# A first mixture of experts whose narrow experts use column halves of the array for the two halves of the weights' columns, with a new class of 32 slots on column quarters

## The chip, the core and the metric

The program runs on one core of one Trainium2 chip. The metric is the device time of one execution in microseconds (us). The times shown are a median of several executions; one more execution was taken with the hardware profiler, and all rows below come from it. TensorE (PE) multiplies, VectorE (DVE), ScalarE (ACT) and GpSimd (POOL) work on elements, SyncE (SP) issues the weight transfers.

## The reference, cut to the first mixture

Three transformer blocks follow each other on 256 tokens of width 1024. The change concerns the mixture of experts of the first: 32 experts, each token goes to its 4 best.

```python
def moe_ffn(h, w_router, b_router, w_mlp1, b_mlp1, w_mlp2, b_mlp2):
    logits = (h @ w_router).astype(jnp.float32) + b_router.astype(jnp.float32)
    top_v, top_i = lax.top_k(logits, TOP_K)                 # 4 of 32 experts
    gates = jax.nn.softmax(top_v, axis=-1)
    ...
    def expert_block(args):
        xb, e = args
        u = xb @ w_mlp1[e] + b_mlp1[e]                      # 1024 -> 2048
        x_glu = jnp.minimum(u[..., ::2], SWIGLU_LIMIT)
        x_lin = jnp.clip(u[..., 1::2], -SWIGLU_LIMIT, SWIGLU_LIMIT)
        a = x_glu * jax.nn.sigmoid(SWIGLU_ALPHA * x_glu) * (x_lin + 1)
        return a @ w_mlp2[e] + b_mlp2[e]                    # 1024 -> 1024
    ...
    out = jnp.zeros((T + 1, D), jnp.float32).at[slot_tok].add(ys.astype(jnp.float32) * slot_gate[:, None])
```

## The kernel before

`moe1` sorts the experts by their number of tokens on the chip (`Order.make`): place 0 is always expert 0, so that its weights can be fetched before routing is known; places 1 to 31 hold the others by falling count. A place has a fixed number of slots: 128 for the first 5 places (wide), 64 for the others (narrow). Should a count exceed its slots, `overflow1` runs a loop over all experts behind a branch.

Each expert has 12 weight tiles of 1 MB (128 x 2048 in fp32): 8 for the up product (two halves of 4) and 4 for the down product. A tile holds two k chunks j of 128 rows with 1024 columns each, and is used as the streamed operand in two column halves n of 512. The gathered tokens x (and later the activations a) are the loaded operand, so an expert with 64 slots fills 64 of the array's 128 columns. In `products` a narrow expert puts the even k chunk on columns 0 to 63 and the odd one on 64 to 127; the two partial sums land on the two halves of the partitions of one PSUM bank, one bank for each n. In `Expert1.act` the result is copied to SBUF (L1562, L1563) and multiplied by `K.fold`, two stacked identities, which transposes it and adds the two partial sums (L1571); a wide expert is transposed plainly (L548). Then comes `swiglu`. `rows` scales the down product by the gate and splits it into yh (L1600) and yl (L1601), and `scatter` multiplies them by the one-hot matrix st (L1330, L1331) and adds the product to the tokens' rows (L1333, L1336), one column half and one half of the tokens at a time.

The experts run in groups: (0), then four groups of one wide and two narrow places, then the rest by fours. For each group `gather` collects the tokens of all its experts by one-hot products (L1292, L1293), during the last expert of the group before. The order on PE, DVE and ACT is written out by hand in `moe1` (a manual schedule): up half 0 of expert e, the last two down tiles of e-1, up half 1, the first two down tiles; `step()` puts one piece of a gather or scatter between two weight tiles, `advance()` puts the next piece of an activation chain between tiles and into the middle of a tile; `weave_all()` finishes what is left at the end of a group. In this stage PSUM has two banks each for u, y, t and the general x.

Weights come through a ring of 12 slots (4 + 4 + 4). SP issues them in program order; each waits until TensorE has used what its slot held. For experts after 0, SP needs the expert's number, which `Order.make` gives at about 228 us. After the last expert the ring shrinks to 4, tiles of the next stage are prefetched, and two of them are split by ACT and DVE (L166, L167) ahead of the last yh.

The order of the groups and the product of a tile stand so before:

```python
WIDE, NARROW, WIDES = 128, 64, 5
CAPS = [WIDE] * WIDES + [NARROW] * (E1 - WIDES)
GROUPS = ([(0,)] + [(n, WIDES + 2 * n - 2, WIDES + 2 * n - 1) for n in range(1, WIDES)]
          + [tuple(range(n, min(n + 4, E1))) for n in range(3 * WIDES - 2, E1, 4)])
```

Of the kernel before, what the change touches and what calls it, by code (L numbers as in the profile page):

```python
# [9 lines left out]
F32 = mybir.dt.float32  # L10
F32R = mybir.dt.float32r
# [3 lines left out]
ALU = mybir.AluOpType  # L15
# [7 lines left out]
P = 128  # L23
# [852 lines left out]
class Residual:  # L876
# [46 lines left out]
    def add(self, x, k):  # L923

        for j in range(2):
# [9 lines left out]
GATHER = 2 * WIDE  # L935
EXTRA = 4


def host2(i):
# [7 lines left out]
    p[:, 34:98] = np.tile(np.eye(64, dtype=np.float32), (2, 1))  # L947
# [193 lines left out]
class Order:  # L1141
# [20 lines left out]
    def make(self, K, tmp, R, b1):  # L1162
# [35 lines left out]
        nc.vector.tensor_scalar(cap, pos, float(CAPS.count(WIDE)), float(WIDE - NARROW), op0=ALU.is_lt, op1=ALU.mult)  # L1198
        nc.vector.tensor_scalar_add(cap, cap, float(NARROW))
# [72 lines left out]
def gather(K, pool, pk, tok, caps, out):  # L1272
# [34 lines left out]
    for e0 in range(0, len(caps), 2):  # L1307
# [5 lines left out]
        for e, cap in some:  # L1313
            slot = K.iota64 if cap == NARROW else K.iota_p
# [6 lines left out]
def scatter(K, out, st, yh, yl):  # L1321

    nc = K.nc
    was = None
    for t in range(2):
        for n in range(2):
            ps = K.bank()
            c = slice(512 * n, 512 * n + 512)
            s = st[:, 128 * t:128 * t + 128]
            nc.tensor.matmul(ps, s, yh[:, c], start=True, stop=False)  # L1330
            nc.tensor.matmul(ps, s, yl[:, c], start=False, stop=True)  # L1331
            if was:
                nc.vector.tensor_add(*was)  # L1333
            was = out[:, t, c], out[:, t, c], ps
            yield
    nc.vector.tensor_add(*was)  # L1336


def moe1(K, x, sums, wr, rp, b1, fill, A2, sh2, gt2, gpost, banks, man, then):
    nc, tc, a = K.nc, K.tc, K.a  # L1340
    with ExitStack() as cs:
        rt = cs.enter_context(tc.tile_pool(name="route", bufs=1))
        out = rt.tile([P, 2, D], F32, name="moe")
        K.fold, K.iota64 = rp[:, 34:98], rp[:, 98:99]
# [175 lines left out]
class Expert1:  # L1520
# [4 lines left out]

    def __init__(self, K, pool, x, gs, b1, cap, advance, w1, w2):
        self.K, self.pool, self.x, self.gs, self.b1, self.cap = K, pool, x, gs, b1, cap
        self.advance, self.w1, self.w2 = advance, w1, w2
        self.parts = P // cap
        self.a = pool.tile([P, KD * WIDE], F32, tag="a", name="a")[:, :KD * cap].rearrange("p (k s) -> p k s", k=KD)  # L1530
        self.acting, self.rowed = set(), False

    def products(self, out, x, q, w):

        m, cap = self.parts, self.cap
        w = w.rearrange("p (k n) -> p k n", k=2)
        for n in range(2):
            for j in range(2):
                k = 2 * q + j
                r = slice(cap * (k % m), cap * (k % m) + cap)  # L1540
                self.K.nc.tensor.matmul(out[n][r], x[:, k], w[:, j, 512 * n:512 * n + 512], start=k < m, stop=k >= KD - m)  # L1541
            if n == 0:
                self.advance()
# [1528 lines left out]
```

## Time and profile before

| what | value |
|---|---|
| median of 3 runs | 2399.83 us (2399.82 to 2401.52) |
| profiled execution | 2405.79 us, span 2403.9 us, mean granted clock 0.972 |
| PE busy | 2291.6 us (95%) |
| DVE busy | 1230.2 us (51%) |
| ACT busy | 814.1 us (34%) |
| read from HBM | 675.82 MB, of which 384 tiles of 1 MB are this mixture's weights |

The profile gives busy time per engine, but the end of a matmul is modelled, so a busy PE is not PE at its peak. The mixture's experts take from about 200 to 1290 us of the span. To see what sets its pace one asks the trace for stretches of it (busy times, granted clock, share and rate of the DMA engines), for who waited for whom, and for the starts of one instruction that each expert has once or twice.

### The profile page before, as it was taken

The numbers are of one execution on the slowest core, as the hardware profiler recorded it, in microseconds if no ns is written. First come the engines' busy times: TensorE is split into PE (matmuls) and PEld (weight loads), VectorE is DVE, ScalarE is ACT, GpSimd is POOL, SyncE is SP. The second block draws the span as 40 slices with busy tenths as digits, with TensorE's granted clock in tenths as the row PEclk, the third lists the DMA queues.
The fourth block names the chain that finished last, engine by engine and source line by source line (L and its number), as shares of the span: only waits on it lengthen the run. The fifth ranks groups of instructions, "written<-read, shape, count | busy, mean of one in ns | idle before, by whom it ended". The sixth has DMA issues, their size and how long they took to land. (4 is left out here: it accounts for less than half of the span.)

```text
span 2403.9 us, 32504 instructions
## 1 busy us (share of the span) xinstructions
PE 2291.6 (95%) x12558; PEld 1449.9 (60%) x12558; DVE 1230.2 (51%) x2303; ACT 814.1 (34%) x1389; POOL 152.9 (6%) x202
## 2 busy tenths in 40 slices
PE   8899999999999999999998888999999998999997
PEld 5775444444443434343435866997889996666664
DVE  5782222222233333323236987887648556566675
ACT  3642010101111111111114674444545435555662
POOL 4000100000000000000000001001000001000000
PEclk8999999999999999999998988999999998999998
DMA  7674898979899999999994523676424445867782
GB/s 273 231 279 190 313 384 302 390 295 360 327 369 423 412 423 405 423 402 423 414 419 168 184 94 144 245 272 257 145 104 177 173 148 215 326 246 278 291 304 90
DMA packets 97845, 680.17 MB, mean 283 GB/s; under 512 B 11776, under 2 KB 14080, under 8 KB 16144
## 3 DMA queue, kind: packets, MB, share of 16 engines
q1 hardware_dynamic: 94752, 671.00, 71.9%
q0 software_dynamic: 2352, 6.44, 0.9%
q8 instruction: 103, 1.69, 0.3%
q10 hardware_dynamic: 576, 0.53, 0.1%
q14 instruction: 62, 0.51, 0.1%
HBM read 675.82 MB, written 2.11 MB: 282 GB/s over the span
## 5 line engine op out<-in xcount | busy, mean ns | idle before, releaser
L1541 PE MATMUL bank<-w,xg 128*64 128x512 f32 (+1 forms) x2048 | 547.1, 601 | 0.0
L167 DVE TENSOR_TENSOR whl<-w,whl 128x1024 fp32r<-128x1024 f32 (+1 forms) x337 | 400.3, 1206 | 175.9 <-ACT whl L166 175.2
L166 ACT CAST whl<-w 128x1024 fp32r<-128x1024 f32 (+1 forms) x347 | 350.5, 1039 | 242.8 <-PE bank L417 100.6
L1541 PEld LDWEIGHTS bank<-w,xg 128*64 128x64 f32 (+1 forms) x2048 | 176.9, 146 | 294.2 <-issue 262.0
L1541 PE MATMUL bank<-w,a 128*64 128x512 f32 (+1 forms) x1024 | 287.4, 605 | 0.0
L1563 DVE COPY us<-bank 128x512 f32<-128x512 f32 x64 | 44.3, 692 | 334.1 <-PE bank L1541 334.1
L1562 ACT COPY us<-bank 128x512 f32<-128x512 f32 x64 | 37.5, 586 | 485.3 <-PE bank L1541 485.3
L1541 PEld LDWEIGHTS bank<-w,a 128*64 128x64 f32 (+1 forms) x1024 | 80.4, 144 | 110.2 <-issue 97.0
L2926 PE MATMUL bank<-whl,xg 128*128 128x512 f32 x512 | 140.8, 404 | 2.1 <-DVE whl L167 2.1
L415 PE MATMUL bank<-hh,whl 128*128 128x256 f32 x448 | 129.1, 288 | 0.0
L417 PE MATMUL bank<-hh,whl 128*128 128x256 f32 x448 | 126.9, 284 | 2.1 <-DVE whl L167 2.1
L416 PE MATMUL bank<-hl,whl 128*128 128x256 f32 x448 | 126.8, 283 | 0.0
L1571 PEld LDWEIGHTS bank<-route_p,us 128*128 128x128 f32 x864 | 100.8, 191 | 42.5 <-issue 36.0
L1620 POOL TENSOR_SCALAR ss<-ss 128x256 f32<-128x256 f32 (+1 forms) x64 | 60.5, 946 | 951.6 <-ACT ss L1617 951.5
L1333 DVE TENSOR_TENSOR moe<-moe,bank 128x512 f32<-128x512 f32 x96 | 65.7, 688 | 105.4 <-PE bank L1331 104.9
L306 DVE SCALAR_TENSOR_TENSOR acc<-w,siluc,acc 128x256 f32<-128x256 f32 x234 | 115.0, 499 | 4.5
L2950 PE MATMUL bank<-w,s 128*64 128x512 f32 x256 | 116.7, 598 | 0.4 <-DVE s L2943 0.4
L417 PE MATMUL bank<-xh,whl 128*128 128x256 f32 x400 | 112.0, 280 | 2.0 <-DVE whl L167 2.0
L415 PE MATMUL bank<-xh,whl 128*128 128x256 f32 x400 | 112.2, 281 | 0.8 <-ACT xh L1834 0.8
L2926 PEld LDWEIGHTS bank<-whl,xg 128*128 128x128 f32 x512 | 89.3, 188 | 38.2 <-DVE whl L167 9.4
L416 PE MATMUL bank<-xl,whl 128*128 128x256 f32 x400 | 112.1, 281 | 0.2 <-DVE xl L1835 0.2
L1571 PE MATMUL bank<-route_p,us 128*128 128x64 f32 x864 | 107.5, 278 | 0.0
(719 smaller groups left out, 3895.9 us busy)
## 6 DMA issues: line engine op xcount, KB each, us to landing
w<-w_mlp SPq DMA_DIRECT2D x384, 1024.0 KB, 9.5
w<-w SPq DMA_DIRECT2D x96, 1024.0 KB, 5.6
w<-w_ada SPq DMA_DIRECT2D x48, 1024.0 KB, 5.0
w<-w_in SPq DMA_DIRECT2D x48, 1024.0 KB, 4.8
w<-w_ff SPq DMA_DIRECT2D x32, 1024.0 KB, 4.8
w<-w_out SPq DMA_DIRECT2D x12, 1024.0 KB, 4.9
w<-cmp_w SPq DMA_DIRECT2D x4, 1024.0 KB, 4.8
w<-w_ret_o SPq DMA_DIRECT2D x4, 1024.0 KB, 4.8
```

Of the source, the lines that this page charges most:

```text
L166: nc.scalar.copy(h, src)
L167: (eng or nc.vector).tensor_tensor(l, src, h.bitcast(F32), op=ALU.subtract)
L306: nc.vector.scalar_tensor_tensor(acc, wv[:, k], self.c[:, k:k + 1], acc, op0=ALU.mult, op1=ALU.add)
L415: nc.tensor.matmul(out, w.h[k][:, c], x.h[:, k], start=first and k == 0, stop=False)
L416: nc.tensor.matmul(out, w.h[k][:, c], x.l[:, k], start=False, stop=False)
L417: nc.tensor.matmul(out, w.l[k][:, c], x.h[:, k], start=False, stop=last and k == nk - 1)
L1333: nc.vector.tensor_add(*was)
L1541: self.K.nc.tensor.matmul(out[n][r], x[:, k], w[:, j, 512 * n:512 * n + 512], start=k < m, stop=k >= KD - m)
L1571: nc.tensor.matmul(ps[:, c], part, K.fold, start=True, stop=True)
L1620: nc.gpsimd.tensor_scalar_min(s, s, 1.0 / (1.0 + math.exp(-1.702 * 7.0)))
L2926: nc.tensor.matmul(self.u, x, part[k], start=q == 0 and k == 0 and n == 0, stop=q == 1 and k == 3 and n == 1)
L2950: nc.tensor.matmul(self.y[n], self.s[:, k], w[:, k, 512 * n:512 * n + 512], start=k == 0, stop=k == 1)
```

## The change

It does four things. In `Expert1.product` a narrow expert puts the column half n = 0 of the weights on columns 0 to 63 of the array and n = 1 on 64 to 127, both with the same k chunk, so that one bank holds everything: partitions 0 to 63 the first 512 columns and 64 to 127 the second. No partial sums are left to add, and the fold becomes a plain transpose. Places 16 to 31 get 32 slots (slim): they use four column quarters, two column halves times two k parities, and a fold by `K.fold32`. `scatter` handles both column halves in a step, for narrow and slim experts with 64 rows each of the contraction. And the groups become (slim, narrow, wide, slim) and (slim, narrow, narrow, slim) in turn, with the last one (slim, narrow, slim).

```diff
-WIDE, NARROW, WIDES = 128, 64, 5
-CAPS = [WIDE] * WIDES + [NARROW] * (E1 - WIDES)
-GROUPS = ([(0,)] + [(n, WIDES + 2 * n - 2, WIDES + 2 * n - 1) for n in range(1, WIDES)]
-          + [tuple(range(n, min(n + 4, E1))) for n in range(3 * WIDES - 2, E1, 4)])
+WIDE, NARROW, SLIM = 128, 64, 32
+WIDES, NARROWS = 5, 11
+CAPS = [WIDE] * WIDES + [NARROW] * NARROWS + [SLIM] * (E1 - WIDES - NARROWS)
...
+    w, n, s = (iter([p for p in range(1, E1) if CAPS[p] == c]) for c in (WIDE, NARROW, SLIM))
+    out = [(0,)]
+    for kinds in [(s, n, w, s), (s, n, n, s)] * 4:
+        out.append(tuple(p for k in kinds for p in [next(k, None)] if p is not None))
...
-    p[:, 34:98] = np.tile(np.eye(64, dtype=np.float32), (2, 1))
+    p[:, 34:98] = np.kron(np.eye(2), np.tile(np.eye(32), (2, 1)))
...
 def scatter(K, out, st, yh, yl):
...
-    was = None
+    was = []
+    halves = yh.shape[-1] < D
     for t in range(2):
+        s = st[:, 128 * t:128 * t + 128]
+        ps = [K.bank() for _ in range(2)]
+        for i, y in enumerate((yh, yl)):
+            for n in range(2):
+                if halves:
+                    r = slice(64 * n, 64 * n + 64)
+                    nc.tensor.matmul(ps[n], s[r], y[r], start=i == 0, stop=i == 1)
+                else:
+                    nc.tensor.matmul(ps[n], s, y[:, 512 * n:512 * n + 512], start=i == 0, stop=i == 1)
         for n in range(2):
-            ps = K.bank()
             c = slice(512 * n, 512 * n + 512)
-            s = st[:, 128 * t:128 * t + 128]
-            nc.tensor.matmul(ps, s, yh[:, c], start=True, stop=False)
-            nc.tensor.matmul(ps, s, yl[:, c], start=False, stop=True)
-            if was:
-                nc.vector.tensor_add(*was)
-            was = out[:, t, c], out[:, t, c], ps
-            yield
-    nc.vector.tensor_add(*was)
+            nc.vector.tensor_add(out[:, t, c], out[:, t, c], ps[n])
+        yield
...
+        self.banks = 2 if cap == WIDE else 1
+        self.parts = 2 if cap == SLIM else 1
...
+    def product(self, out, x, w, n, k):
+
+        m, cap = self.parts, self.cap
+        r = 0 if self.banks == 2 else 64 * n + cap * (k % m)
+        self.K.nc.tensor.matmul(out[n % self.banks][r:r + cap], x[:, k], w[:, k % 2, 512 * n:512 * n + 512],
+                                start=k < m, stop=k >= KD - m)
+
     def products(self, out, x, q, w):
 
-        m, cap = self.parts, self.cap
         w = w.rearrange("p (k n) -> p k n", k=2)
-        for n in range(2):
-            for j in range(2):
-                k = 2 * q + j
-                r = slice(cap * (k % m), cap * (k % m) + cap)
-                self.K.nc.tensor.matmul(out[n][r], x[:, k], w[:, j, 512 * n:512 * n + 512], start=k < m, stop=k >= KD - m)
-            if n == 0:
+        for j in range(2):
+            for n in range(2):
+                self.product(out, x, w, n, 2 * q + j)
+            if j == 0:
                 self.advance()
...
-            nc.scalar.copy(us[:, 0], u[0])
-            nc.vector.tensor_copy(us[:, 1], u[1])
+            for n in range(self.banks):
+                (nc.scalar.copy, nc.vector.tensor_copy)[n](us[:, n], u[n])
...
-                        nc.tensor.matmul(ps[:, c], part, K.fold, start=True, stop=True)
+                        nc.tensor.matmul(ps[n][:, 64 * c:64 * c + 64], part, K.fold32, start=True, stop=True)
```

The order on PE, for a narrow expert before that neither begins nor ends a group: the rest of its turn from the fold of up half 0 on. L1541 is the product, L1571 the fold, L1330 and L1331 the scatter of the expert before.

```order
L1541 MATMUL bank<-w,xg 64x512 x16
L1541 MATMUL bank<-w,a 64x512 x2
L1571 MATMUL bank<-route_p,us 128x64 x8
L1541 MATMUL bank<-w,a 64x512 x6
L1541 MATMUL bank<-w,xg 64x512 x8
L1330 MATMUL bank<-yh,st 128x512
L1331 MATMUL bank<-yl,st 128x512
L1541 MATMUL bank<-w,xg 64x512 x4
L1330 MATMUL bank<-yh,st 128x512
L1331 MATMUL bank<-yl,st 128x512
L1541 MATMUL bank<-w,xg 64x512 x4
```

The same place on PE in the changed kernel, for a slim expert. L1558 is the product, L1595 the fold, L1349 and L1351 the scatter.

```order
L1558 MATMUL bank<-w,xg 32x512 x16
L1558 MATMUL bank<-w,a 32x512 x2
L1595 MATMUL bank<-route_p,us 128x64 x4
L1558 MATMUL bank<-w,a 32x512 x6
L1558 MATMUL bank<-w,xg 32x512 x8
L1349 MATMUL bank<-yh,st 128x512 x2
L1349 MATMUL bank<-yl,st 128x512 x2
L1558 MATMUL bank<-w,xg 32x512 x4
L1349 MATMUL bank<-yh,st 128x512 x2
L1349 MATMUL bank<-yl,st 128x512 x2
L1558 MATMUL bank<-w,xg 32x512 x4
```

The products stand in the same number and places; the fold has 4 matmuls instead of 8, and the scatter comes in two pieces of four instead of four pieces of two.

The order on ACT over two narrow experts before, with us the copy of an up half and ss the sigmoid:

```order
L1562 COPY us<-bank 128x512
L1617 ACTIVATE ss<-sg 128x256
L1600 ACTIVATE yh<-bank,gs 128x512 x2
L1562 COPY us<-bank 128x512
L1617 ACTIVATE ss<-sg 128x256
L1562 COPY us<-bank 128x512
L1617 ACTIVATE ss<-sg 128x256
L1600 ACTIVATE yh<-bank,gs 128x512 x2
```

And in the changed kernel, where one slim expert follows another:

```order
L1588 COPY us<-bank 128x512
L1645 ACTIVATE ss<-sg 128x128
L1628 ACTIVATE yh<-bank,gs 128x512
L1588 COPY us<-bank 128x512
L1645 ACTIVATE ss<-sg 128x128
```

One yh stands where two stood, and the sigmoid of a slim expert is half as long.

## Rows read from the trace of the kernel before

**Rows 1.** Stretches: length, busy time (instructions) by engine, granted clock, DMA share, GB/s.

```profile
core 0: us, PE busy (x) PEld busy (x) DVE busy (x) ACT busy (x) POOL busy (x), PEclk, DMA share, GB/s
228.00:1260.00 1032.00, 1024.88 (x4701) 445.64 (x4702) 308.94 (x604) 132.55 (x259) 86.47 (x125) 0.99 0.95 381
270.00:300.00 30.00, 30.00 (x86) 14.57 (x85) 9.90 (x15) 3.22 (x5) 3.71 (x4) 1.00 0.70 247
750.00:780.00 30.00, 30.00 (x147) 11.79 (x143) 9.07 (x17) 3.38 (x6) 2.50 (x4) 1.00 1.01 423
```

**Rows 2.** Waits in the stage: engine, line, waited for: us, times, longest.

```profile
SPq L134 <- PE bank L1541: 785.4, 363, 17.5
PEld bank L1541 <- DMA w<-w_mlp: 12.4, 37, 0.8
```

**Rows 3.** Timeline of ACT, some starts of yh: start, us, engine, instruction [idle before].

```profile
277.84 0.69 ACT L1600 ACTIVATE yh<-bank,gs 128x512 fp32r<-128x512 f32 x1 [2.46 <-PE bank L1541]
...
539.14 0.69 ACT L1600 ACTIVATE yh<-bank,gs 128x512 fp32r<-128x512 f32 x1 [3.45 <-PE bank L1541]
...
649.46 0.69 ACT L1600 ACTIVATE yh<-bank,gs 128x512 fp32r<-128x512 f32 x1 [3.45 <-PE bank L1541]
...
959.44 0.69 ACT L1600 ACTIVATE yh<-bank,gs 128x512 fp32r<-128x512 f32 x1 [1.83 <-PE bank L1541]
...
987.45 0.69 ACT L1600 ACTIVATE yh<-bank,gs 128x512 fp32r<-128x512 f32 x1 [1.84 <-PE bank L1541]
...
1015.47 0.69 ACT L1600 ACTIVATE yh<-bank,gs 128x512 fp32r<-128x512 f32 x1 [1.84 <-PE bank L1541]
...
1081.71 0.69 ACT L1600 ACTIVATE yh<-bank,gs 128x512 fp32r<-128x512 f32 x1 [1.83 <-PE bank L1541]
```

**Rows 4.** Timeline of PE, expert 0 (wide): products, transposes, products.

```profile
242.16 1.88 PE L1541 MATMUL bank<-w,a 128*128 128x512 f32 x4
243.87 1.04 PE L548 MATMUL bank<-ident,us 128*128 128x128 f32 x8
244.75 1.88 PE L1541 MATMUL bank<-w,a 128*128 128x512 f32 x4
```

**Rows 5.** Timeline of PE and of its weight loads (PEld), a narrow expert.

```profile
1000.29 1.08 PE L1541 MATMUL bank<-w,a 128*64 128x512 f32 x4
...
1004.59 0.14 PEld L1541 LDWEIGHTS bank<-w,xg 128*64 128x64 f32 x2 [0.29 <-issue]
1005.02 0.14 PEld L1541 LDWEIGHTS bank<-w,xg 128*64 128x64 f32 x2 [0.29 <-issue]
```

**Rows 6.** Timeline of PE, narrow experts: a scatter piece and the next product, a fold.

```profile
1001.30 0.50 PE L1330 MATMUL bank<-yh,st 128*128 128x512 f32 x1
...
1001.96 1.51 PE L1541 MATMUL bank<-w,a 128*64 128x512 f32 x6
...
1010.60 1.03 PE L1541 MATMUL bank<-w,a 128*64 128x512 f32 x4
1011.55 2.00 PE L1571 MATMUL bank<-route_p,us 128*128 128x64 f32 x16
1013.48 1.08 PE L1541 MATMUL bank<-w,a 128*64 128x512 f32 x4
```

**Rows 7.** Timeline at the end of the stage: the second prefetched tile's casts, the last yh.

```profile
1279.42 1.99 ACT L166 CAST whl<-w 128x1024 fp32r<-128x1024 f32 x2 [6.76 <-issue]
...
1281.32 1.26 ACT L1600 ACTIVATE yh<-bank,gs 128x512 fp32r<-128x512 f32 x2
```

**Rows 8.** SP's first issue behind routing, issues from 228 us on, a stretch as in rows 1.

```profile
228.54 32.99 SPq L134 DMA_DIRECT2D w<-w_mlp  x14
...
w<-w_mlp SPq DMA_DIRECT2D x374, 1024.0 KB, 9.5
...
250.00:260.00 10.00, 10.00 (x42) 4.71 (x41) 2.21 (x5) 0.00 (x0) 0.00 (x0) 1.00 1.01 426
```

**Rows 9.** A stretch of the next block with TensorE half idle, as in rows 1.

```profile
1460.00:1480.00 20.00, 10.91 (x45) 8.32 (x43) 16.97 (x23) 5.93 (x9) 9.61 (x4) 0.76 0.44 158
```

More of the change, by code (lines that the diff above doesn't have):

```diff
@@ L1313, in gather @@
         for e, cap in some:
-            slot = K.iota64 if cap == NARROW else K.iota_p
+            slot = {WIDE: K.iota_p, NARROW: K.iota64, SLIM: K.iota_32}[cap]
             if pk.base == 0:
@@ L1550, in up @@
             if q == 0:
-                self.u = [K.bank("u" if "u" in K.ps else "x") for _ in range(2)]
+                self.u = [K.bank("u" if "u" in K.ps else "x") for _ in range(self.banks)]
             self.products(self.u, self.x, q, w)
@@ L1561, in steps @@
             us = self.pool.tile([P, 2, 512], F32, tag="us", bufs=1, name="us")
-            nc.scalar.copy(us[:, 0], u[0])
-            nc.vector.tensor_copy(us[:, 1], u[1])
+            for n in range(self.banks):
+                (nc.scalar.copy, nc.vector.tensor_copy)[n](us[:, n], u[n])
             yield
-            tr = []
-            for n in range(2):
-                ps = K.bank("t" if "t" in K.ps else "x")[:, :4 * cap].rearrange("p (c s) -> p c s", c=4)
+            ps = [K.bank("t" if "t" in K.ps else "x") for _ in range(self.banks)]
+            for n in range(self.banks):
                 for c in range(4):
@@ L1570, in steps @@
                     if self.parts > 1:
-                        nc.tensor.matmul(ps[:, c], part, K.fold, start=True, stop=True)
+                        nc.tensor.matmul(ps[n][:, 64 * c:64 * c + 64], part, K.fold32, start=True, stop=True)
                     else:
-                        transpose_to(K, ps[:, c], part)
-                tr.append(ps)
+                        transpose_to(K, ps[n][:, 128 * c:128 * c + 128], part)
+            if self.banks == 2:
+                tr = [p.rearrange("p (c s) -> p c s", c=4) for p in ps]
+            else:
+                tr = ps[0][:, :8 * cap].rearrange("p (c n s) -> p c n s", c=4, n=2)
+                tr = [tr[:, :, n] for n in range(2)]
             yield
@@ L1588, in down @@
         if q == 0:
-            self.yp = [K.bank("y" if "y" in K.ps else "x") for _ in range(2)]
+            self.yp = [K.bank("y" if "y" in K.ps else "x") for _ in range(self.banks)]
         self.products(self.yp, self.a, q, w)
@@ L1596, in steps @@
         def steps():
-            yh, yl = self.y = [self.pool.tile([P, D], F32R, tag=n, bufs=1, name=n) for n in ("yh", "yl")]
-            for n in range(2):
+            yh, yl = self.y = [self.pool.tile([P, D], F32R, tag=n, bufs=1, name=n)[:, :512 * self.banks] for n in ("yh", "yl")]
+            for n in range(self.banks):
                 c = slice(512 * n, 512 * n + 512)
@@ L1634, in overflow1 @@
             with tc.For_i(0, E1) as e:
-                for base in range(0, T - NARROW, WIDE):
+                for base in range(0, T - SLIM, WIDE):
                     pk = PickAt(K, pool, R, ctr, base, cap)
```

13 lines of the change are left out of this document (9 added, 4 removed).

## The prediction

> **What bounds the kernel now.** I read the stretches of the expert stage first, then the waits, then the starts of one activation per expert, then single rows of TensorE. The stage from 228 to 1260 us moves 381 GB/s at a DMA share of 0.95, but that is a mean of two halves: where a wide expert runs the stream falls to 247 GB/s, share 0.70; among narrow ones it holds 423 GB/s, share 1.01, which I take as the ceiling, since nothing in this stage goes visibly above it for long [rows 1]. The waits say who holds whom: the queue that issues weights waited 785 us, 363 times, for TensorE to hand a ring slot back, while TensorE's weight loads waited 12.4 us for weights in the whole stage [rows 2]. So TensorE sets the pace, even in the half where the stream looks full. The starts of yh agree: two narrow experts are 28.0 us apart (987.45 to 1015.47), whereas 12 tiles at 1.0486 MB and 423 GB/s take 12 x 2.479 = 29.7 us; narrow experts live off tiles that piled up in the 12-slot ring while a gather or a wide expert ran [rows 1, 3].
>
> **TensorE's prices, from rows.** A matmul with fp32 operands leaves two records; one pass over 512 columns takes 0.43 us. On the full array four records took 242.16 to 243.87, 1.71 us, so a wide tile (8 records) is 3.43 us [rows 4]. On column halves two loads start every 0.43 us, and after a pause four records took 1.08 us in all: two passes, each of two at once; a narrow tile is 1.71 us [rows 5]. A block of 16 fold records costs 1013.48 - (1010.60 + 0.86) = 2.0 us, the 8 transposes of a wide expert 244.75 - 243.87 = 0.9 us, one scatter piece 1001.96 - (1000.29 + 0.86) = 0.8 us [rows 4, 6]. A narrow expert before: 12 x 1.71 + 2 x 2.0 + 4 x 0.8 = 27.8; measured 28.0. Four narrow ones with a gather take 1081.71 - 959.44 = 122.3, so the gather is 122.3 - 112.1 = 10.2. One wide, two narrow and a gather take 649.46 - 539.14 = 110.3, so a wide one is 44.1 [rows 3].
>
> **The change part by part.**
> *Halves of the weights' columns on halves of the array.* The number of passes of a narrow tile is the same, 1.71 us. What goes is what follows: one bank instead of two, so 4 transposes per half instead of 8 folds (half of 0.9 plus the switch, about 0.6 us instead of 2.0), one yh, yl and us each instead of two, and two scatter steps instead of four. A step now has four matmuls, on two row halves. Bounds per step from 0.8 (the halves overlap fully) to 1.6 (they don't); I take 1.2. A narrow expert: 20.6 + 1.2 + 2.4 = 24.2 us. The copies on ACT and DVE that fall away cost nothing now and save nothing: VectorE is busy 309 of 1032 us [rows 1].
> *The added wait.* The scatter's additions no longer lag by one piece, so VectorE waits right behind the four matmuls, with the swiglu steps of the next expert queued behind it, and both general PSUM banks are taken until its two additions are done. Lower bound nothing (a weight tile lies between two steps), upper bound two additions of about 0.7 us (the yh row of the same size: 0.69 [rows 3]) twice per expert, 31 x 2.8 = 87 us of TensorE. I take nothing, as only the last expert of a group runs its steps back to back; the slack below covers the 87 too.
> *The class of 32.* No row of before shows column quarters. If four matmuls run at once, as two do on halves, a tile is 0.86 us; the upper end is 3.43, one after the other as in [rows 4]. I take 0.86, since halves start pairwise without loss and the two passes of one matmul do not hold up its neighbour [rows 5]. To 12 x 0.86 = 10.3 come two tiles that the fold splits (2 x 0.86), two folds of half the records (1.1 each) and the scatter, 2.4: 16.6 us. The Trainium skill ("TensorE: Matmul & The Clock Gate", "Measured speedup vs the span model") gives 2.38 times for three column tiles; scaled to four, an estimate by that page, a slim tile would be 1.08 us, 2.6 us more per slim expert and the total the same, since the weights still come later.
> *Capacity.* I counted the router's choices on the reference's inputs: behind expert 0, which has place 0, the counts are 88, 76, 72, 64, then 60 down to 29 for eleven, then 28 and less. Nothing exceeds 128, 64 or 32, so the overflow loop stays off.
> *The order.* Wide experts now have slim and narrow neighbours; there is one group less.
>
> **The sum.** After expert 0, TensorE needs 16 x 16.6 + 11 x 24.2 + 4 x 44.1 + 7 gathers x 10.2 = 266 + 266 + 176 + 71 = 779 us. Before, by the same prices: 27 x 28.0 + 4 x 44.1 + 8 x 10.2 = 1014, where the rows have 1281.32 - 277.84 = 1003.5 [rows 3, 7]; the prices are 1% high. The stream needs 31 x 29.7 = 922 us, so it takes over. When routing is known SP issues 374 tiles from 228.54 on, and the stream is full from then [rows 8]: 228.5 + 2 + 374 x 2.479 = 1157.7 for the last landing. Early on TensorE and stream are level: slim, narrow, wide, slim and a gather need 16.6 + 24.2 + 44.1 + 16.6 + 10.2 = 112 us against 119, with the ring still full from expert 0; I allow 3 us lost there (0 to 8). Later the deficit of a wide expert, 14 us or 6 tiles, fits in the ring. At the end the last yh waits for two prefetched tiles behind the last weights (2 x 2.48) and the second one's two casts (2.0 [rows 7]): 7 us, and the tail behind it is 1 us shorter. The last yh moves from 1281.3 to 1157.7 + 3 + 7 = 1167.7; with the 1 us, 114.6 us go. The profiled execution would be 2405.8 - 114.6 = 2291; its time is 6 us over the median of 2399.8, so I predict **2285 us**. A cross-check: raising 381 to 423 GB/s over 1032 us gives 102 us, and the rest is TensorE's backlog behind the last landing.
>
> **The rivals.**
> *Two at a time.* If quarters give no more than halves, a slim expert is 20.6 + 2.2 + 2.4 = 25.2, TensorE needs 917 us against the stream's 922, and neither covers the other's uneven places. With some 10 us for that, the last yh comes near 1200: 2318 us. For it: no row shows four. Against: [rows 5].
> *One at a time, the slower end.* If quarters shut each other out, a slim tile costs 3.43 us and the slim expert 45.8; TensorE then needs 733 + 513 = 1246 us, the last yh is at 267.6 + 1246 = 1513 (expert 0 ends 10 us earlier, since the four tiles in between shrink from 13.7 to 3.4 us), and the kernel takes 2632 us. It decides from a slim expert of 31 us on, that is (31.0 - 4.6) / 12 = 2.2 us per tile, where TensorE's sum reaches the 1013 us it has today. Against it: halves overlap [rows 5].
> *The clock.* TensorE will now stand idle part of each slim tile, 0.86 us of work in 2.48. In before a stretch with 10.9 of 20 us busy had a mean granted clock of 0.76 [rows 9], so part of it ran at the lower level of 1.2 GHz; the busy stretches of the stage have 1.00 [rows 1]. At 0.76 a slim expert takes 21.8 us and the sum 862, still under 922: no change. At one and a half times its price, 24.9 us, it comes to the 2318 us of above; at the lower level throughout (33.2 us) to 1045, slower than today, but then TensorE would be busy without a pause. The Trainium skill ("TensorE: Matmul & The Clock Gate", "HAM oscillation") speaks against the change here: matmul bursts shorter than the wait for their next weights fall back to the half rate each time. Of that the trace shows the low clock in a half-idle stretch, not its cost under a weight stream.
> *No gain.* The ceiling of 423 GB/s could fall when up to 11 tiles are in flight instead of the few of today; to lose all, it would have to fall to 381. From 250 to 260 us, behind the first issues after routing, it was 426 [rows 8].
>
> **How the numbers follow.** Stream-bound 0.74, at 2285: from 2272 (426 GB/s saves 6.5, nothing lost early 3, a tail of 4 instead of 7) to about 2300 (8 lost early, steps and waits at their upper ends). Two at a time 0.10 and the clock 0.08, both near 2318; one at a time 0.05; no gain 0.03. A range from 2272 to 2322 holds most of the first three. A measurement of this kernel can tell about 0.2%, 5 us, from no change. Faster 0.92, same 0.03, slower 0.05.
>
> **What would show it.** Right: the stage holds 423 GB/s from 240 us to its end without the falls to 247; TensorE's waits for weights grow from 12 us to over 100, while SP waits far less for TensorE; yh starts are evenly about 30 us apart; four loads of 32 columns start within one 0.43 us pass; the last yh is near 1168. Wrong: slim tiles of 1.7 us or more with TensorE still waited for, long stretches at half clock with the stream below 423, or an overflow loop that runs.

## The result, and the profile after

| | before | after |
|---|---|---|
| median, us | 2400.68 (4 runs, 2399.82 to 2404.02) | **2300.53** (4 runs, 2297.52 to 2304.63) |
| ratio, 95% interval | | 0.9582 (0.9563 to 0.96) |
| profiled execution, us | 2405.79, span 2403.9 | 2297.52, span 2295.7 |
| PE / DVE / ACT busy, us | 2291.6 / 1230.2 / 814.1 | 2089.4 / 1146.2 / 787.0 |

The kernel is 100 us faster, 4.2%. The prediction was 2285 us, 2272 to 2322; it missed by 15.5 us inside its range. In the sections below the padding and buffer experiments look for these 15 us, the others take the change apart.

Stretches of the changed kernel, to be read beside [rows 1] (length, busy time and instructions of PE, PEld, DVE, ACT, POOL, granted clock, DMA share, GB/s):

```profile
core 0: us, PE busy (x) PEld busy (x) DVE busy (x) ACT busy (x) POOL busy (x), PEclk, DMA share, GB/s
228.00:1160.00 932.00, 837.30 (x4297) 312.67 (x4295) 227.38 (x515) 106.07 (x224) 74.04 (x124) 0.97 1.01 419
270.00:300.00 30.00, 30.00 (x157) 10.00 (x157) 9.24 (x19) 3.58 (x7) 3.11 (x6) 1.00 1.01 418
360.00:420.00 60.00, 58.58 (x364) 21.52 (x358) 17.19 (x39) 6.96 (x15) 4.93 (x10) 0.94 1.00 412
```

Where the stream fell to 247 GB/s it now moves 418; the whole stage has a DMA share of 1.01 and 419 GB/s, against 0.95 and 381. TensorE, which was busy 1024.88 of 1032 us, is busy 837 of 932. Only a short part, 360 to 420, sinks to 412.

The waits from 228 to 1200 us, to be read beside [rows 2] (who, for whom, us in total, times, longest):

```profile
SPq L134 <- DMA w<-w_mlp: 526.9, 284, 12.0
SPq L134 <- PE bank L1558: 194.8, 131, 7.6
...
PEld bank L1558 <- DMA w<-w_mlp: 140.9, 136, 2.8
...
PE bank L1558 <- DMA w<-w_mlp: 88.2, 116, 1.9
```

The sides have changed. The issuing queue waited 785 us for TensorE; now that is 195 us, and 527 us go to transfers ahead of it. TensorE's weight loads waited 12.4 us for weights; now they wait 141 us, and the products 88 us. A weight tile needs 19.8 us from issue to landing instead of 9.5 [rows 8], with nothing slower: more tiles stand in the queue.

The slim experts' products on column quarters. First the weight loads (PEld) of a stretch in which the tiles already lie in the ring, then PE where each tile is awaited (start, us, engine, instruction, count of records, idle before):

```profile
480.41 0.20 PEld L1558 LDWEIGHTS bank<-w,xg 128*32 128x32 f32 x4 [0.66 <-issue]
481.26 0.20 PEld L1558 LDWEIGHTS bank<-w,xg 128*32 128x32 f32 x4 [0.66 <-issue]
482.12 0.20 PEld L1558 LDWEIGHTS bank<-w,xg 128*32 128x32 f32 x4 [0.66 <-issue]
...
484.39 0.12 PEld L1558 LDWEIGHTS bank<-w,xg 128*32 128x32 f32 x4 [0.37 <-issue]
484.82 0.11 PEld L1558 LDWEIGHTS bank<-w,a 128*32 128x32 f32 x2 [0.31 <-issue]
485.25 0.11 PEld L1558 LDWEIGHTS bank<-w,a 128*32 128x32 f32 x2 [0.32 <-issue]
```

```profile
486.20 1.10 PE L1595 MATMUL bank<-route_p,us 128*128 128x64 f32 x8
...
490.70 1.07 PE L1558 MATMUL bank<-w,xg 128*32 128x512 f32 x8 [0.70 <-DMA w<-w_mlp]
491.70 0.49 PE L1349 MATMUL bank<-yh,st 64*128 64x512 f32 x2
492.03 0.39 PE L1349 MATMUL bank<-yl,st 64*128 64x512 f32 x2
493.20 1.07 PE L1558 MATMUL bank<-w,xg 128*32 128x512 f32 x8 [0.78 <-DMA w<-w_mlp]
494.20 0.50 PE L1349 MATMUL bank<-yh,st 64*128 64x512 f32 x2
494.53 0.40 PE L1349 MATMUL bank<-yl,st 64*128 64x512 f32 x2
495.70 1.07 PE L1558 MATMUL bank<-w,xg 128*32 128x512 f32 x8 [0.77 <-DMA w<-w_mlp]
```

```profile
479.50:484.00 4.50, 4.50 (x25) 1.17 (x28) 1.52 (x4) 0.00 (x0) 0.00 (x0) 0.50 1.01 419
484.50:490.00 5.50, 5.50 (x44) 1.95 (x34) 0.58 (x3) 1.58 (x3) 0.81 (x2) 1.00 1.02 423
490.00:500.00 10.00, 6.33 (x44) 2.04 (x44) 3.72 (x7) 0.58 (x1) 0.00 (x0) 1.00 1.01 419
```

Four loads start together, and the next ones follow 0.43 us later (484.39 to 484.82, the latter the two of a product that the fold splits). In the single records of the trace the four matmuls of a pass start within 21 ns, and two passes of four stand 0.43 us apart at the full clock (484.384 and 484.814). A tile has eight records, two passes of four, so it costs 0.86 us, as predicted; a tile that was awaited holds TensorE for 1.0 us (490.70 to 491.70). The fold of eight records takes 1.03 us (486.20 to 487.23, where the next product starts), where [rows 6] have 2.0 for sixteen. From 480.41 on the step is 0.855 us, twice that of the full clock: the three stretches show why, a granted clock of 0.50 up to 484.0 (the lower level, 1.2 GHz) and 1.00 behind it. From 490.70 on the tiles come every 2.5 us, and the products wait for each of them.

The starts of yh, the first of expert 0's and then one per narrow or slim expert, beside [rows 3], and the end of the stage, beside [rows 7] (the last expert's last product on PE, then ACT; start, us):

```profile
266.79 0.69 ACT L1628 ACTIVATE yh<-bank,gs 128x512 fp32r<-128x512 f32 x1 [3.65 <-PE bank L1558]
...
638.01 0.69 ACT L1628 ACTIVATE yh<-bank,gs 128x512 fp32r<-128x512 f32 x1 [0.92 <-PE bank L1558]
668.84 0.69 ACT L1628 ACTIVATE yh<-bank,gs 128x512 fp32r<-128x512 f32 x1 [1.80 <-PE bank L1558]
699.15 0.69 ACT L1628 ACTIVATE yh<-bank,gs 128x512 fp32r<-128x512 f32 x1 [2.04 <-PE bank L1558]
729.29 0.69 ACT L1628 ACTIVATE yh<-bank,gs 128x512 fp32r<-128x512 f32 x1 [1.16 <-PE bank L1558]
758.20 0.69 ACT L1628 ACTIVATE yh<-bank,gs 128x512 fp32r<-128x512 f32 x1 [0.93 <-PE bank L1558]
```

```profile
1169.70 1.07 PE L1558 MATMUL bank<-w,a 128*32 128x512 f32 x8 [1.34 <-DMA w<-w_mlp]
...
1172.17 1.99 ACT L166 CAST whl<-w 128x1024 fp32r<-128x1024 f32 x2 [7.14 <-DMA w<-w_in]
1174.71 1.99 ACT L166 CAST whl<-w 128x1024 fp32r<-128x1024 f32 x2 [0.55 <-issue]
1176.60 0.68 ACT L1628 ACTIVATE yh<-bank,gs 128x512 fp32r<-128x512 f32 x1
```

Four experts take 758.20 - 638.01 = 120.2 us, and 48 tiles of 1.0486 MB at 419 GB/s take 120.1. The last weight tile is used at 1169.7, as soon as it has landed; each of the two prefetched tiles is converted when it lands, and the last yh starts at 1176.6 instead of 1281.3.

### The profile page after: what moved, and what is told of

Same layout as the page of the kernel before. It is cut to its first block, busy times and chain, and to the rows that moved or that the text cites. A ratio compares the mean times of both kernels' runs of the same rounds, so it can differ in the third digit from the quotient of the medians.

```text
span 2295.7 us, 31455 instructions
## 1 busy us (share of the span) xinstructions
PE 2089.4 (91%) x12134; PEld 1308.6 (57%) x12134; DVE 1146.2 (50%) x2222; ACT 787.0 (34%) x1354; POOL 140.8 (6%) x202
## 5 line engine op out<-in xcount | busy, mean ns | idle before, releaser
L1558 PE MATMUL bank<-w,xg 128*32 128x512 f32 (+2 forms) x2048 | 460.4, 626 | 65.1 <-DMA w<-w_mlp 65.1
L1558 PEld LDWEIGHTS bank<-w,xg 128*32 128x32 f32 (+2 forms) x2048 | 131.1, 135 | 323.8 <-issue 192.9
L1558 PE MATMUL bank<-w,a 128*32 128x512 f32 (+2 forms) x1024 | 256.7, 609 | 23.2 <-DMA w<-w_mlp 23.2
L1643 DVE TENSOR_TENSOR sg<-bank,b1cols 128x128 f32<-128x128 f32 (+2 forms) x64 | 25.6, 400 | 360.1 <-PE bank L1595 198.4
L1558 PEld LDWEIGHTS bank<-w,a 128*32 128x32 f32 (+2 forms) x1024 | 67.5, 132 | 140.5 <-issue 94.6
L1354 DVE TENSOR_TENSOR moe<-moe,bank 128x512 f32<-128x512 f32 x128 | 82.3, 684 | 118.3 <-PE bank L1349 107.5
L417 PEld LDWEIGHTS bank<-hh,whl 128*128 128x128 f32 x448 | 84.8, 189 | 3.1 <-DVE whl L167 3.1
L415 PEld LDWEIGHTS bank<-hh,whl 128*128 128x128 f32 x448 | 85.2, 190 | 0.9 <-issue 0.6
L416 PEld LDWEIGHTS bank<-hl,whl 128*128 128x128 f32 x448 | 85.2, 190 | 0.6 <-issue 0.5
## 6 DMA issues: line engine op xcount, KB each, us to landing
w<-w_mlp SPq DMA_DIRECT2D x384, 1024.0 KB, 19.8
```

The lines of the kernel that those rows point to most:

```text
L415: nc.tensor.matmul(out, w.h[k][:, c], x.h[:, k], start=first and k == 0, stop=False)
L416: nc.tensor.matmul(out, w.h[k][:, c], x.l[:, k], start=False, stop=False)
L417: nc.tensor.matmul(out, w.l[k][:, c], x.h[:, k], start=False, stop=last and k == nk - 1)
L1354: nc.vector.tensor_add(out[:, t, c], out[:, t, c], ps[n])
L1558: self.K.nc.tensor.matmul(out[n % self.banks][r:r + cap], x[:, k], w[:, k % 2, 512 * n:512 * n + 512], start=k < m, stop=k >= KD - m)
L1643: nc.vector.tensor_tensor(o, ps, v.rearrange("p (c a) -> p c a", a=1).broadcast_to([P, 4, cap]), op=ALU.add)
```

## The experiments

Each ratio is to the kernel before as it ran beside the experiment; its medians there were 2403.3 to 2404.4 us.

**Without the class of 32.** The two layouts of the products taken apart: places 16 to 31 keep 64 slots and column halves; the order of places stays (cut anew where a group would pass 256 slots).

```diff
-CAPS = [WIDE] * WIDES + [NARROW] * NARROWS + [SLIM] * (E1 - WIDES - NARROWS)
+CAPS = [WIDE] * WIDES + [NARROW] * (E1 - WIDES)
```

> The changed kernel without the class of 32: places 16 to 31 get 64 slots again and use column halves; the order of the places stays, in groups of at most 256 slots. If the weight stream is the bound and TensorE only has to stay below it, TensorE needs 27 x 24.2 + 4 x 44.1 + 8 x 10.2 = 911 us behind expert 0 against 31 x 30.1 = 933 of the stream, so the time is that of the changed kernel or up to 15 us more where the two are uneven: 2300 to 2315 us. If the quarters carry the gain, by 16 x 7.6 = 122 us less work on TensorE, it comes back toward 2400: 2380 to 2400 us.

2322.96 us, ratio 0.9655 (0.9638 to 0.9671). Its rows, two narrow experts that follow each other and a long stretch:

```profile
998.11 0.69 ACT L1632 ACTIVATE yh<-bank,gs 128x512 fp32r<-128x512 f32 x1 [1.80 <-PE bank L1562]
1021.81 0.69 ACT L1632 ACTIVATE yh<-bank,gs 128x512 fp32r<-128x512 f32 x1 [1.80 <-PE bank L1562]
```

```profile
600.00:1000.00 400.00, 394.63 (x1772) 148.66 (x1773) 101.49 (x224) 49.94 (x102) 35.77 (x54) 0.97 1.00 413
```

A narrow expert costs 1021.81 - 998.11 = 23.7 us where 24.2 was predicted and 28.0 stood before. TensorE is busy 395 of 400 us again and the stream falls to 413: both near their bound, neither covering the other's uneven places. That is the state that the prediction priced at 2318 us ("two at a time", there for another reason). So column halves in the new order of places bring some 81 us (2404.4 - 2323.0), and the class of 32 another 22 (2323.0 - 2300.5); the expected 2300 to 2315 was 8 us short. What halves bring in the old order was not run.

**The order of places alone, in the kernel before.**

```diff
-GROUPS = ([(0,)] + [(n, WIDES + 2 * n - 2, WIDES + 2 * n - 1) for n in range(1, WIDES)]
-          + [tuple(range(n, min(n + 4, E1))) for n in range(3 * WIDES - 2, E1, 4)])
+GROUPS = grouped()    # the order of the changed kernel, groups cut at 256 slots
```

> The kernel before with nothing changed but the order: its wide experts spread among narrow ones as in the changed kernel, in groups of at most 256 slots. If TensorE's sum is what counts, it is 27 x 28.0 + 4 x 44.1 + 9 x 10.2 = 1024 us as before, and the time stays at 2395 to 2410 us. If the bunched wide experts were the loss, the stream runs full and the time falls to some 2310 to 2330 us.

2405.92 us, ratio 1.0007 (0.9997 to 1.0016). The 400 us stretch and the queue's wait:

```profile
600.00:1000.00 400.00, 397.46 (x1835) 171.98 (x1837) 122.63 (x235) 51.77 (x99) 34.50 (x50) 1.00 0.94 378
```

```profile
SPq L134 <- PE bank L1556: 798.4, 367, 17.0
```

TensorE still has no free time, and the queue waits 798 us for it: spreading wide experts is worth nothing while TensorE's sum is the bound.

**The changed kernel with the groups of before.**

```diff
-GROUPS = grouped()
+GROUPS = ([(0,)] + [(n, WIDES + 2 * n - 2, WIDES + 2 * n - 1) for n in range(1, WIDES)]
+          + [tuple(range(n, min(n + 4, E1))) for n in range(3 * WIDES - 2, E1, 4)])
```

> The changed kernel with the groups of before: four groups of one wide and two narrow, then narrow and slim ones by fours. TensorE's sum is nearly that of the changed kernel. If only the sum counts: 2300 us. If the ring's 12 tiles are what evens things out, a group of 44.1 + 2 x 24.2 + 10.2 = 102.7 us against 90.3 of the stream falls 12.4 us behind, four times, with the ring full from expert 0 on: some 45 us lost, 2340 to 2350 us, and the slim half later can't win it back, since the stream is full there already.

2367.28 us, ratio 0.9838 (0.9822 to 0.9855). The wide part, the rest, and two yh of the same place in groups that follow each other:

```profile
228.00:640.00 412.00, 408.04 (x1499) 172.54 (x1500) 100.98 (x203) 46.89 (x93) 39.57 (x46) 0.98 0.88 347
640.00:1240.00 600.00, 490.15 (x2893) 168.09 (x2889) 131.37 (x333) 61.61 (x142) 37.31 (x82) 0.87 1.01 417
```

```profile
388.35 0.69 ACT L1629 ACTIVATE yh<-bank,gs 128x512 fp32r<-128x512 f32 x1 [1.76 <-PE bank L1559]
...
495.27 0.69 ACT L1629 ACTIVATE yh<-bank,gs 128x512 fp32r<-128x512 f32 x1 [1.76 <-PE bank L1559]
```

One wide and two narrow experts with a gather take 106.9 us of TensorE, and their 36 tiles 36 x 2.503 = 90.1 us of stream. Four such groups lose 4 x 16.8 = 67 us, which is what was measured (2367.3 - 2300.5). By the prediction's prices such a group is 44.1 + 2 x 24.2 + 10.2 = 102.7 us; the 4 us that it really takes more, four times, are most of what the expectation was short of. The TensorE time that the slim experts save comes behind 640 us, where the stream is full anyway. The same order that brought nothing alone is worth 67 us in the changed kernel; without it halves and quarters together bring only 37 us (2404.4 - 2367.3).

**Half of the scatter's products left out.** The products with yl are missing, so the low parts of the experts' rows don't reach the output.

```diff
-        for i, y in enumerate((yh, yl)):
+        for i, y in enumerate((yh,)):
```

> The changed kernel with the low parts' products left out of the scatter (the 4 matmuls with yl of each expert), so some 0.4 us twice per expert, 25 us of TensorE's work, are gone. If the stream is the bound: the same time within 5 us, 2295 to 2305. If TensorE still holds the stage: 2275.

2297.75 us, ratio 0.9557 (0.9541 to 0.9573), an interval that meets the changed kernel's. The stage:

```profile
228.00:1160.00 932.00, 831.37 (x4178) 302.50 (x4176) 228.13 (x514) 106.08 (x224) 74.05 (x124) 0.96 1.01 419
```

There are 119 records of products fewer, and the stream is the same 419 GB/s; by the trace's records of landings a tile takes 2.517 us in both kernels. Some 25 us of TensorE's work are gone and at most 3 us of time: TensorE's work is no longer on the path.

**Expert 0's last two tiles early.** If the stream bounds the stage from its first tile, two tiles fewer in it are 5 us.

```diff
+                    if e == 0:
+                        ahead = [new.w2(2), new.w2(3)]
...
-                        old.down(q, rest[q - 2] if e == E1 else None)
+                        old.down(q, rest[q - 2] if e == E1 else ahead[q - 2] if e == 1 else None)
```

> Expert 0 is the only one whose weights are known before the routing. The changed kernel asks for ten of its twelve weight tiles before the stage's stream begins and for the last two behind expert 1's; this one asks for those two ahead of expert 1's as well, in time in which the queue has nothing else to move. If the stage is bound by its stream from the first tile to the last, two tiles of 2.51 us leave it: the stage ends 5.0 us sooner, 2300.5 - 5.0 = 2295.5 us (2293 to 2298). If something else than the stream sets the end (the products, or the tail behind the last tile), nothing changes: 2300 us.

A miss: 2308.56 us, ratio 0.961 (0.9596 to 0.9623) where the changed kernel has 0.9582, some 7 us slower; the intervals just meet. The queue's longest wait in the first 42 us of the stream and the stretch:

```profile
SPq L134 <- PE bank L1560: 34.3, 8, 10.2
```

```profile
230.00:270.00 40.00, 40.00 (x202) 18.46 (x204) 10.90 (x21) 5.99 (x13) 3.43 (x4) 1.00 0.75 296
```

All 12 buffers now hold expert 0's tiles when routing is known, and the next transfer waits 10.2 us until TensorE has used the first; the stream starts at 296 GB/s, where the changed kernel has 421. 125 GB/s less over 40 us are 11.9 us, and the two tiles spared give 5.0 back; the last weight tile lands 5.9 us later (1175.6 against 1169.7). At its start the stage is bound by free buffers, not by the count of tiles.

**Six buffers instead of twelve.**

```diff
-EXTRA = 4
+EXTRA = 2
...
-        K.ring.add(K.hlpool, HL)
```

> The changed kernel with 6 buffers for the stream instead of 12 (the four that the splitting of other stages' weights uses, and two of the four added for the mixture, are not lent to it). It tells what the buffers are worth now. The prediction assumed that a ring of 12 tiles carries the stream over the wide clusters, which hold TensorE for up to 35 us while 30 us of tiles land. If that is so, six tiles (15 us of stream) don't cover them and the start (six of expert 0's tiles early, not ten): four wide stretches lose some 5 us each and the start four tiles, 10 us: 2300.5 + 30 = 2330 us (2315 to 2345). If the buffers are not what carries the stream: 2300 us. Its stream has gaps again, so if gaps bring the packets back to 309 ns, more than half of them should be at 309 ns here.

2338.14 us, ratio 0.9733 (0.9716 to 0.9751), as expected. The start, a wide expert's stretch, and the queue:

```profile
230.00:270.00 40.00, 40.00 (x200) 18.63 (x199) 10.52 (x20) 6.22 (x14) 3.42 (x4) 1.00 0.73 269
300.00:360.00 60.00, 58.88 (x210) 24.95 (x207) 13.79 (x30) 5.65 (x11) 6.76 (x8) 1.00 0.93 376
```

```profile
SPq L134 <- PE bank L1557: 690.0, 366, 8.6
```

The changed kernel has 420 GB/s from 300 to 360. So it is the ring that carries the stream over the wide experts, as the prediction assumed. Of its packets in the stage 22% took 309 ns, where the changed kernel has 9%: gaps bring some of them back, but not the half that was expected.

**The conversion of the next stage's tiles behind the last rows.** The call of `K.presplit` for the two prefetched tiles moves from ahead of `old.rows()` to behind them.

> In the changed kernel the last expert's queue of work on VectorE and ScalarE holds the conversion of the next stage's first two tiles ahead of the last expert's output rows; here that conversion stands behind them, and nothing else differs. Between the landing of the last expert tile (1166 to 1169 us) and the last output row (1176.6 us) lie 7 to 10 us; the conversions of two tiles are 3 to 4 us of it if the row waits for them. Theory: the tail is work in series behind the last tile, and the time falls by 3 to 4 us, to 2296.5 to 2297.5 us. Rival: the next stage needs those two tiles just as early, and what the row gains its first products lose: 2300 us, with the last row earlier by 3 to 4 us all the same.

2302.97 us, ratio 0.9582 (0.9569 to 0.9596). The rival holds:

```profile
1170.02 0.69 ACT L1628 ACTIVATE yh<-bank,gs 128x512 fp32r<-128x512 f32 x1 [5.87 <-PE bank L1558]
1171.28 1.99 ACT L166 CAST whl<-w 128x1024 fp32r<-128x1024 f32 x2 [0.57 <-DMA w<-w_in]
```

The last yh comes 6.6 us sooner, and what lies behind it is 5.2 us longer (2294.3 - 1170.0 against 2295.7 - 1176.6). The row no longer stands behind the two tiles and their casts, but the next stage waits for the same casts: they only change places.

**32 bytes of padding.** The packets of the stream were longer than before; one difference between the kernels is where the buffers lie.

```diff
+        self.pad = self.const.tile([P, 8], F32, name="pad")
+        nc.vector.memset(self.pad, 0.0)
```

> The changed kernel with 32 bytes more in the pool of constants, set to zero and used by nothing: every buffer behind it in SBUF lies 32 bytes further on. The 12 buffers that the stream fills lie at 32 past a multiple of 64 bytes in the changed kernel, and at multiples of 64 here; in the kernel before four of the twelve did so. Its packets of 8192 bytes took 309 ns at best, those of the changed kernel 313 to 320 ns. Theory A: where a packet lands decides that; all packets go to 309 ns, a tile from 2.508 to about 2.479 us, and 374 tiles save 374 x 0.029 = 11 us: 2289.5 us (2286 to 2293). Theory B: the longer packets come from the stream being full without a break (or from the engines reading at the same time), and the place does nothing: 313 ns and 2300 us (2298 to 2303).

2296.14 us, ratio 0.9556 (0.9543 to 0.9569). The two were then run side by side:

> The changed kernel as it is, on the chip on which the aligned one runs again, so that the two can be set against each other: 2300.5 us, the ratio to the kernel before 0.958.

> The changed kernel with the 32 bytes of padding once more. Its packets were 1 ns shorter (312 and 319 ns instead of 313 and 320 ns) and its tiles landed every 2.501 us instead of 2.508 us, which is 2.4 us over the 324 tiles between the first and the last of the quiet part, 2.6 us over all 374. Theory A (this is real, and all of it): 2.4 us less than the unpadded kernel beside it, a ratio of 0.957. Theory B (the 4 us that lay between the medians were the chips'): the same time as the unpadded kernel.

Unpadded 2301.5 us, ratio 0.9578 (0.9565 to 0.9591); padded 2298.76 us, ratio 0.9567 (0.9554 to 0.958). One row of each, unpadded first:

```profile
600.00:1000.00 400.00, 349.61 (x1881) 124.79 (x1880) 94.94 (x224) 43.91 (x93) 29.38 (x54) 0.95 1.01 419
```

```profile
600.00:1000.00 400.00, 347.46 (x1887) 123.43 (x1887) 95.99 (x226) 44.70 (x94) 29.85 (x55) 0.96 1.01 421
```

421 instead of 419 GB/s. From the first to the last landing a whole tile takes 2.509 instead of 2.517 us, in both pairs of runs, which is 3.2 us over the stage; the medians are 2.7 us apart. The intervals of the times meet, but the landings repeat: the padding is worth some 3 us, and 11 were expected. The packets went from 313 and 320 to 312 and 319 ns, not to 309.

Where the 309 ns come from is only narrowed down. In the kernel before, the share of 309 ns packets, sorted by the buffer's address in SBUF (packets of 28 or 29 tiles each, from the records of the trace):

```
address     past a multiple of 256   share at 309 ns
140544       0                       0.86
165120       0                       0.98
156928       0                       0.97
148736       0                       0.91
27168       32                       0.94
35360       32                       0.88
43552       32                       0.62
18976       32                       0.52
51744       32                       0.46
76320       32                       0.42
68128       32                       0.45
59936       32                       0.47
```

The rows stand in the order in which the ring is filled. The four buffers at multiples of 256 bytes have nearly all their packets at 309 ns; the two filled behind them still do, and it fades from there. In the changed kernel, whose buffers all lie 32 past a multiple of 256, the share is 0.09, and with the padding, which put them 64 past one, 0.11. Gaps play a part too: the changed kernel with the old groups has 0.52 up to 640 us, where its stream has gaps, and 0.10 behind. But they don't make the pattern by address: in that part its twelve buffers, all at 32, have 0.40 to 0.66, and none stands out as the four do above. This fits a cause at 256 bytes with an after-effect on the next few tiles, and 64, the multiple that the experiment chose, was then the wrong one. The Trainium skill ("DMA: Bandwidth & Descriptors", "How a descriptor splits into AXI transactions") has bursts of 256 bytes that must start at multiples of 256, for reading; it doesn't say this of the place written. Buffers at multiples of 256 in the changed kernel were not tried, so the cause stays open.

**All three together.** Expert 0's last tiles early, the conversion moved, and the padding.

> All three edits together: expert 0's last two tiles early, the conversion of the next stage's tiles behind the last rows, and the 32 bytes. If each of them pays for itself and none takes the other's place: 5 + 3.5 + 11 us, 2300.5 - 19.5 = 2281 us (2276 to 2286). If the place of the buffers does nothing: 2292 us. If neither the tail nor the place matters: 2295.5 us.

2302.36 us, ratio 0.958 (0.9566 to 0.9593), a miss. It is 6.2 us under the kernel with the early tiles alone, but above the padded one: the first 40 us of the stream again run at 308 GB/s, and what the other two give doesn't make up for that.

**Each tile by two transfers of 64 partitions**, on top of the padding.

```diff
-        self.nc.sync.dma_start(out=w, in_=src)
+            self.nc.sync.dma_start(out=w[:64], in_=src[:64])
+            self.nc.sync.dma_start(out=w[64:], in_=src[64:])
```

> The padded kernel, in which each weight tile of the mixture's stream is fetched by two transfers of 64 partitions instead of one of 128 (twice the issues, each with half the packets, the same bytes). In the kernel before, the packets of a tile that followed a gap took 309 ns, and after some tiles in a row without a gap they turned to 313 and 320 ns; in the changed kernel, whose stream has no gaps, they stayed there. Theory A: the 16 engines fall into a step in which they hinder each other, and another order of partitions over time brings another step: packets differ from 312 and 319 ns, and the tile from 2.501 us, by 1% either way (2.479 us would give 2288 us). Theory B: the rate is what SBUF or HBM take from a full stream, whatever its order: 2.50 us, 2298 us. Against both: if an issue of a transfer costs the stream something, the tile gets longer, and the dwell of the issuing queue shows it.

2861 to 2972 us (4 runs) beside 2403.41 of the kernel before: at least 19% slower than before, outside of everything expected. A stretch, and the issues from 230 to 600 us with their KB and time to landing:

```profile
230.00:270.00 40.00, 40.00 (x190) 19.10 (x188) 10.53 (x23) 5.69 (x13) 3.42 (x4) 1.00 1.01 216
```

```profile
w<-w_mlp SPq DMA_DIRECT2D x159, 512.0 KB, 19.1
```

The engines are just as busy (share 1.01) and move half: 216 instead of 423 GB/s, with 603 ns for a packet of 8192 bytes, on the mean from 230 to 600 us, instead of 314. The engines have no pauses, so it isn't the doubled number of issues that costs; each packet takes longer. It looks as if the packets of one half hindered each other and the two halves didn't run beside each other. The Trainium skill ("SBUF — State Buffer", "Door 1: The DMA port swizzle (why `[64,N]` ≈ `[32,N]`)") says that partitions 0 to 63 reach 8 of SBUF's 16 ports and 64 to 127 the other 8; a transfer to one half then gets half the rate. The measured 216 agrees. Why the rate later rises (286 GB/s from 600 to 1000 us) wasn't followed up. That cutting a tile across the partitions costs is shown; smaller transfers of 128 partitions were not tried beside it, and whether an order exists that beats 128 at a time is open.

## Why the prediction was right, and where its sum was off

**The bound.** TensorE set the pace before: order alone gave nothing, and halves in that same order, which lower TensorE's sum and leave the stream's tiles as they are, gave 81 us. The stream sets it now: half of the scatter's products left out change nothing, and four experts take the time of their 48 tiles. Both halves of the first step hold.

**Prices.** A slim tile 0.86 us: measured 0.86. A narrow expert 24.2: measured 23.7, in the kernel without the class of 32. First yh at 267.6: measured 266.8. The added wait of the scatter, taken as nothing, is there: the scatter's weight loads waited 29.7 us for VectorE's additions from 228 to 1200 us. Under a full stream it costs no time. A scatter step of four products on row halves, bounded by 0.8 and 1.6 us and taken at 1.2: 0.72 by the modelled ends (491.70 to 492.42), so the halves overlap. Under a full stream that price doesn't count any more.

**The stream's rate was the mis-sized term.** The step that took 423 GB/s, 2.479 us a tile, from a 30 us stretch of before [rows 1] and put it on all 374 tiles was too good. By the trace's records of landings the first tile landed at 230.67 and the last at 1169.66, one every 2.517 us: 373 x 0.0384 = 14.3 us. Two things are in it. The bytes came at 419 GB/s, 2.503 us a tile: the stretch of before had 53% of its packets at 309 ns and most of the others at 313 to 320, the changed kernel has 9% of the first. And the landing of a tile is recorded in 16 steps, of which the last counts. It came 0.35 us behind the first step at the first tile and 7.8 us behind it at the last; in the kernel before, whose stream has gaps, never more than 3.5. So the parts of a tile drift apart in a stream without a break, as if the slowest of the 16 engines fell ever further behind, and its pace is the tile's. The rate of the bytes, which the prediction used, doesn't show that. The floor of the range, 426 GB/s, was further off still.

**Start and early loss.** The first tile landed 2.3 us sooner than the sum's 228.5 + 2 + 2.5 = 233.0; the same kernel run again had it at 233.0, so this is not the change's. The 3 us allowed for a dip are not needed beside the measured spacing, which holds it (60 x 7 / 419 = 1.0 us from 360 to 420 us). Together 14.3 - 2.3 - 3.0 = 9.0 us: the last weight tile landed at 1169.66, and the sum had 1160.7.

**The tail** was sized rightly. 7 us were put behind the last weights: two tiles of 2.48 us and one tile's casts of 2.0. The two tiles landed at 1172.15 and 1174.64, the second one's casts started at 1174.71, and yh at 1176.60: 6.9 us. So yh starts 8.9 us behind the predicted 1167.7, and all of it is the stream's. The rest of the kernel got 3.5 us shorter, where 1 was assumed. And the experiment with the moved conversion shows that the tail is not free to take: the next stage waits for the same casts.

**The basis.** By profiled executions 2405.8 - 2297.5 = 108.3 us went, 6.3 short of the 114.6. The other 9 us of the miss are none of the change: the profiled run of before stood 6 us above its median and that of after 3 us below, so a subtraction from the former carried over 6 us, and 3 more, of which the early start is 2.3. There is some luck in the 6.3: the rate alone cost 14.3 us, and the early start, the allowance of 3 us and the shorter rest gave 8 of them back.

**The rivals.** Two at a time and one at a time: four loads start together at either clock. The clock: the level did fall, in nine stretches from 228 to 1160 us, 58 us in all, and the rows show one of them, at 0.50 from 479.5 to 484.0, with a pass at 0.855 us instead of 0.43. It cost nothing, since by 490.70 TensorE waited for tiles again. Seven of the nine lie behind a change of group, where small products of the gather and the scatter stand (474 to 479 us has 0.83); the other two, from 733 and from 1146 us, lie behind slim tiles of about 1 us with waits of 1.3 to 1.9 us. The rule of the Trainium skill ("TensorE: Matmul & The Clock Gate", "HAM oscillation") that bursts shorter than their waits fall back each time came about in part. It did in these two, and more in the experiment with the old groups, where slim experts follow one another: 0.87 from 640 to 1240 us, with the stream at 417 GB/s all the same. From 490 to 500 us, where TensorE is busy 6.3 of 10 us and its waits are 0.7 to 1.4 us, the granted clock is 1.00. The 2.38 times for three column tiles of the Trainium skill ("TensorE: Matmul & The Clock Gate", "Measured speedup vs the span model") are not what these rows show for four: the same 0.43 us for one pass of four as for one.

```profile
474.00:479.00 5.00, 3.56 (x29) 2.08 (x28) 3.10 (x7) 0.00 (x0) 0.00 (x0) 0.83 1.02 424
```

**The signs.** Of those named ahead, the even spacing of yh was put too simply: 12 tiles take 30 us on the mean (638.01 to 758.20), but single steps run from 28.9 to 30.8 there, and further in wide groups, since the ring lends and takes back.

## What to carry to other kernels

When an edit takes work off the engine that sets the pace, look for the next bound, and price it by a stretch as long as the one on which it will act: 30 us at 2.479 us a tile were 1.5% too good for 930 us at 2.517, and only whole landed tiles show that, not the rate of the bytes. An order that spreads heavy pieces is worth nothing under one bound (2405.9 against 2404.4) and 67 us under the next, so test it again after each change of bound. Buffers that a prefetch fills are missing when the stream starts (the last weight tile 5.9 us later for two tiles fetched earlier), and a transfer cut across the partitions can halve the rate (216 against 423 GB/s).

## What the runs showed of the hardware that was not expected

- The sixteen parts of a tile drift apart in a stream without a break: the last came 0.35 us behind the first at the start and 7.8 us after 374 tiles, at a DMA share of 1.01; in the kernel before, whose stream has gaps, it was never more than 3.5 us.
- Transfers into 64 partitions instead of 128, two of them in the same queue one behind the other, ran at half the rate up to 600 us: 603 ns a packet instead of 314, at the same share of busy DMA engines.
- Packets of 8192 bytes have sharp lengths, 309, 313 and 320 ns; the share at 309 was 0.52 where the stream had gaps and 0.10 where it had none, in the same run, and 32 bytes of padding made 312 and 319 of the other two.
- Four products with 32 columns start within 21 ns, pass by pass, and each pass of the four costs 0.43 us at the full clock and 0.855 us at half of it.
